# Sixteen short score matmuls of the sample rows, spread over the K tiles of projection block u6

## The chip, the cores and the metric

The kernel runs on one core of one Trainium2 chip. The time is that of one launch on the device, in microseconds (us). The engines named here are PE (the TensorE matmul; PEld is its weight load, which is recorded apart), DVE (VectorE), ACT (ScalarE), POOL (GpSimd) and SP (SyncE, which issues nearly all DMAs here, in order). Each engine works through its own list of instructions and waits on semaphores for the others.

## What is computed

One step of a decoder layer for a prompt group (16 meta tokens and 512 prompt positions) and for a sample group (8 rows, one new position each, with a cache of 128 keys and values per row). Cut to what matters:

```python
def mixer_inputs(h, pos, w_in, b_in):            # h: 2048 wide
    z = jnp.einsum('btd,de->bte', h, w_in) + b_in
    q, k, v, u = ...                             # 16 heads x 64, 4 x 64, 4 x 64, pool input 1024
    return partial_rope(q, pos), partial_rope(k, pos), v, u

def sink_attention(q, k, v, mask, sinks):
    s = jnp.einsum('...qhgd,...shd->...hgqs', q, k) * (1.0 / math.sqrt(HEAD_DIM))
    s = jnp.where(mask, s, NEG_INF)
    m = jnp.maximum(jnp.max(s, -1, keepdims=True), sink)
    p = jnp.exp(s - m)
    denom = jnp.sum(p, -1, keepdims=True) + jnp.exp(sink - m)
    return jnp.einsum('...hgqs,...shd->...qhgd', p / denom, v)

hs = layer_norm(x_sample, ...)
qs, ks_, vs, us = mixer_inputs(hs, pos_s, w_in[l], b_in[l])
k_all = jnp.concatenate([cache_k[l], ks_], 1)    # 128 cached keys and the new one
a_s = sample_window_attention(qs, k_all, v_all, pos_s, sinks)
```

After the mixer come the pooling branch, the output projection, a layer norm, a SwiGLU feed-forward block and a second layer norm, the same for both groups. The prompt rows and the sample rows share every large matmul: the 536 columns of a projection are 16 meta tokens, 8 sample rows and 512 prompt positions.

## The kernel before

All large products are computed in two float32r parts: a weight tile is split into `wh` (its rounded part, ACT, line 187) and `wl` (the rest, DVE, line 188), the activations likewise, and `products` issues wh·hi (L203), wh·lo (L204) and wl·hi (L206). Such a matmul is called wide below: a 128x128 weight against 276 or 260 columns. Small products, among them everything of attention, are plain float32 matmuls; the trace shows each of them as two passes.

The first stage (to about 350 us) makes the input projection. `in_block` computes 128 output features for all 536 columns: it takes two PSUM banks (276 and 260 columns) and calls `full_block`, which walks over the 2048 inputs in 16 K tiles; a K tile is six wide matmuls. Blocks q0 to q7 are query heads, u0 to u7 the pool input. Between the blocks stand the turns of attention. For turn t the program issues the values of turn t-1 (`att_values`, L609), the scores (`att_scores`, L547), one or two projection blocks, then the transposes of the softmax (`att_turn`, L591 to L598). The softmax runs on DVE and ACT meanwhile.

The sample rows' attention is a generator, `sample_attention`, cut into pieces by `yield`. Its first piece loads the cached keys (two tiles of 128x1024, `kct`) and makes the scores: for each of 8 rows and 2 halves of the heads, one matmul with a 128x128 tile of keys as weight and only 8 query columns (L697), 16 in all, into one PSUM bank `smT`. ACT copies the bank to SBUF (L699). Later pieces transpose it (L708), make the softmax, load the cached values (`vc`) and multiply by them with 32 short matmuls of 4 columns (L742).

`with step(pe)` fixes the order of groups on PE: what is issued in one step comes after what the step before issued. Within a step, and on the other engines, a scheduler orders the instructions. The loads of weights, of `kct` and of `vc` go through one ring of five raw tiles in the order in which the program asks for them; the two `vc` tiles come into the places of the two `kct` tiles. A place is free again when its last reader is done.

In turn 6 the first piece of `sample_attention` is asked for right behind the scores of the prompt; then block u6 follows:

```python
sc = att_scores(t, qs.pop(t))
if t >= 6:
    next(sample)
```

## Time and profile before

| | us |
|---|---|
| three timed runs | 1918.43, 1920.60, 1920.91 (median 1920.6) |
| the profiled execution, its own time | 1923.03 |
| span of its trace, first to last instruction | 1921.2 |
| PE busy in the span | 1890.5 (98%) |
| DVE busy | 1537.7 (80%) |
| ACT busy | 957.6 (50%) |
| mean granted clock of PE | 0.993 |

The trace belongs to the profiled execution alone, which took 2.43 us more than the median of the timed runs. Its times start at the first instruction. PE's busy time is modelled: a matmul is shown from its start to the end of its pipeline, so back-to-back matmuls overlap in the record, and what one costs is read from the distance of two starts. The granted clock (PEclk) is the share of full speed that TensorE was allowed in a stretch.

### The profile page before, as it was taken

What the parts mean: (1) busy time and instruction counts of PE and PEld (TensorE: products, weight loads), DVE (VectorE), ACT (ScalarE), POOL (GpSimd) and SP (SyncE); (2) the same over time, 40 slices, a digit from 0 to 9 for tenths busy, and PEclk for the clock granted to TensorE, in tenths of its full rate; (3) what the DMA queues carried; (4) which work ended last, traced back from release to release, by engine and by line L of the source; (5) the groups of instructions that cost most, each with busy time, mean ns of one, the idle gap of its engine ahead of it and who ended that gap; (6) DMA issues with size and microseconds to landing.
All of it is one profiled execution on the core that took longest, in us unless ns stands there. A gap on an engine that the chain in (4) does not pass through costs nothing.

```text
span 1921.2 us, 39215 instructions
## 1 busy us (share of the span) xinstructions
PE 1890.5 (98%) x15533; PEld 1862.9 (97%) x15533; DVE 1537.7 (80%) x2734; ACT 957.6 (50%) x1808; POOL 2.7 (0%) x9
## 2 busy tenths in 40 slices
PE   8999999999999999999999999999999999999996
PEld 8999999999989999999999999999999999999996
DVE  6666667768777988988898888888877888888878
ACT  6644445545654555555555555555555433434341
POOL 0000000000000000000000000000000000000000
PEclk9999999999999999999999999999999999999998
DMA  8722222665745455454545344453568655645332
GB/s 281 233 99 68 70 75 71 206 207 193 251 153 176 150 171 172 148 183 145 176 149 172 128 164 151 153 169 127 178 243 322 233 197 178 219 166 191 94 100 90
DMA packets 145240, 319.27 MB, mean 166 GB/s; under 512 B 14288, under 2 KB 66232, under 8 KB 144952
## 3 DMA queue, kind: packets, MB, share of 16 engines
q1 hardware_dynamic: 144480, 315.71, 49.6%
q8 instruction: 122, 2.00, 0.4%
q10 hardware_dynamic: 576, 1.05, 0.2%
q14 instruction: 62, 0.51, 0.1%
HBM read 265.22 MB, written 54.03 MB: 166 GB/s over the span
## 4 chain that ended last, share of the span: by engine, by line
PE 92%; DVE 3%; DMA 2%; ACT 2%; issue 1%; SPq 0%; DVEq 0%; ACTq 0%
PE p_g L203 8%; PE p_g L204 8%; PE p_g L206 8%; PE p_u L203 7%; PE p_u L206 7%; PE p_u L204 7%; PE tri L203 6%; PE tri L206 6%; PE tri L204 6%; PE o L203 3%; PE o L206 3%; PE o L204 3%; PE p_u L1003 2%; PE mm_u L203 2%; PE mm_u L206 2%; PE mm_u L204 2%
## 5 line engine op out<-in xcount | busy, mean ns | idle before, releaser
L187 ACT CAST rr<-fr 128x512 fp32r<-128x512 f32 (+1 forms) x1056 | 669.9, 644 | 738.3 <-DVE fr L196 151.5
L188 DVE TENSOR_TENSOR rr<-fr,rr 128x512 fp32r<-128x512 f32 (+1 forms) x1056 | 743.7, 715 | 244.2 <-ACT rr L187 233.8
L196 DVE TENSOR_TENSOR fr<-fr 128x1024 f32<-128x1024 f32 (+1 forms) x304 | 319.2, 1050 | 4.9 <-DMA fr<-in_w_g_dram 4.3
L203 PE MATMUL p_g<-rr 128*128 128x260 f32 x830 | 234.1, 283 | 0.0
L206 PE MATMUL p_g<-rr 128*128 128x260 f32 x830 | 230.2, 282 | 0.0
L204 PE MATMUL p_g<-rr 128*128 128x260 f32 x788 | 221.4, 282 | 0.0
L203 PE MATMUL p_u<-rr 128*128 128x260 f32 x770 | 217.8, 283 | 0.6 <-ACT fr L1044 0.6
L206 PE MATMUL p_u<-rr 128*128 128x260 f32 x770 | 214.7, 281 | 0.0
L204 PE MATMUL p_u<-rr 128*128 128x260 f32 x748 | 210.5, 282 | 0.0
L206 PE MATMUL tri<-rr 128*128 128x260 f32 x696 | 196.7, 283 | 1.8 <-DVE rr L188 1.8
L203 PE MATMUL tri<-rr 128*128 128x260 f32 x696 | 197.1, 283 | 0.8 <-ACT rr L187 0.8
L204 PE MATMUL tri<-rr 128*128 128x260 f32 x696 | 196.7, 283 | 0.0
L203 PEld LDWEIGHTS p_g<-rr 128*128 128x128 f32 x830 | 156.1, 188 | 0.0
L206 PEld LDWEIGHTS p_g<-rr 128*128 128x128 f32 x830 | 155.1, 189 | 0.0
L204 PEld LDWEIGHTS p_g<-rr 128*128 128x128 f32 x788 | 148.1, 188 | 0.0
L203 PEld LDWEIGHTS p_u<-rr 128*128 128x128 f32 x770 | 144.8, 188 | 0.8 <-ACT fr L1044 0.8
L203 PE MATMUL o<-rr 128*128 128x260 f32 x512 | 145.0, 284 | 0.3 <-ACT rr L187 0.3
L206 PEld LDWEIGHTS p_u<-rr 128*128 128x128 f32 x770 | 144.4, 189 | 0.0
L204 PE MATMUL o<-rr 128*128 128x260 f32 x512 | 144.0, 282 | 0.0
L206 PE MATMUL o<-rr 128*128 128x260 f32 x512 | 143.6, 282 | 0.2 <-DVE rr L188 0.2
L204 PEld LDWEIGHTS p_u<-rr 128*128 128x128 f32 x748 | 140.6, 188 | 0.0
L206 PEld LDWEIGHTS tri<-rr 128*128 128x128 f32 x696 | 131.3, 189 | 2.6 <-DVE rr L188 2.6
(320 smaller groups left out, 4563.2 us busy)
## 6 DMA issues: line engine op xcount, KB each, us to landing
fr<-in_w_u_dram SPq DMA_DIRECT2D x100, 512.0 KB
fr<-in_w_g_dram SPq DMA_DIRECT2D x90, 512.0 KB
fr<-in_w_d_dram SPq DMA_DIRECT2D x64, 640.0 KB
t_d<-fr SPq DMA_DIRECT2D x140, 260.0 KB
fr<-in_w_o_dram SPq DMA_DIRECT2D x64, 512.0 KB
fr<-in_w_in_dram SPq DMA_DIRECT2D x48, 512.0 KB
rr<-t_d SPq DMA_DIRECT2D x87, 260.0 KB
mid_b<-t_d SPq DMA_DIRECT2D x53, 260.0 KB
```

Source lines behind the costliest of these rows:

```text
L187: nc.scalar.copy(wh, s)
L188: last_lo[0] = (lo or nc.vector).tensor_sub(wl, s, wh.bitcast(F32)).ins
L196: i = op(*args).ins
L203: nc.tensor.matmul(o, wh, hi[j], start=first, stop=False, skip_group_check=onto)
L204: nc.tensor.matmul(o, wh, lo[j], start=False, stop=False, skip_group_check=onto)
L206: nc.tensor.matmul(o, wl, hi[j], start=False, stop=last, skip_group_check=onto)
L1003: nc.tensor.matmul(bk, self.q(0, n - 1)[:, k * P:(k + 1) * P], z1[0][4 * (n - 1) + k // 2][:, k % 2, :], start=(k == 0), stop=(k == 7))
```

## The change

`full_block` takes an optional generator `side` and advances it once behind each K tile. `u_block` and `in_block` pass it on, and only block u6 is given one: `sample`. The first piece of `sample_attention` is cut up: one `yield` stands behind the loads of the keys, and one behind each of the 16 score matmuls. So the call in turn 6 that made all scores now only asks for the keys, the 16 K tiles of u6 then each issue one score matmul, and a new call behind block u6 issues the copy of `smT` and the short products on DVE. The value products (L742) stay one run.

```diff
-    def full_block(src, name, out, hi, lo, low=None, apart=False):
+    def full_block(src, name, out, hi, lo, low=None, apart=False, side=None):
...
                          k == 0, k == KT - 1)
+                if side is not None:
+                    next(side)
...
                    for i in range(2)]
+            yield
             st_ = aux_tile([P, 2, 8, NS], "pt", "smT", 1)
             for b in range(NS):
                 kc = kcs[b // 4][:, b % 4]
                 for t4 in range(2):
                     ts = slice(4 * t4, 4 * t4 + 4)
                     nc.tensor.matmul(st_[:, :, ts, b], kc[:, t4, :], qd[:, :, ts, b], start=True, stop=True)
+                    yield
...
-                    us.append(u_block(int(n[1]), n == "u7"))
+                    us.append(u_block(int(n[1]), n == "u7", sample if n == "u6" else None))
...
             block(names[0])
+            if t == 6:
+                next(sample)
             with step(pe):
                 if t < 7:
                     att_turn(t)
```

In the changed file, line numbers are larger by 2 to 6 (L697 becomes L700, L699 becomes L703).

The order of PE before, from the last prompt scores of turn 6 (`sc`) over the short scores (`smT`) into block u6 (`mm_u`):

```order
L547 MATMUL sc_1_0_3256<-mid_a 128x256
L547 MATMUL sc_1_1_3257<-mid_a 128x256
L697 MATMUL smT<-fr 128x2x4 x16
L203 MATMUL mm_u_0_3326<-rr 128x276
L204 MATMUL mm_u_0_3326<-rr 128x276
L203 MATMUL mm_u_1_3327<-rr 128x260
L204 MATMUL mm_u_1_3327<-rr 128x260
L206 MATMUL mm_u_0_3326<-rr 128x276
L206 MATMUL mm_u_1_3327<-rr 128x260
L203 MATMUL mm_u_0_3326<-rr 128x276
```

The same place of PE after the change:

```order
L549 MATMUL sc_1_0_3256<-mid_a 128x256
L549 MATMUL sc_1_1_3257<-mid_a 128x256
L203 MATMUL mm_u_0_3305<-rr 128x276
L204 MATMUL mm_u_0_3305<-rr 128x276
L203 MATMUL mm_u_1_3306<-rr 128x260
L204 MATMUL mm_u_1_3306<-rr 128x260
L206 MATMUL mm_u_0_3305<-rr 128x276
L206 MATMUL mm_u_1_3306<-rr 128x260
L700 MATMUL smT<-fr 128x2x4
L203 MATMUL mm_u_0_3305<-rr 128x276
```

The run of 16 ahead of the block is gone; one short matmul stands behind every six wide ones, the last of them behind the last K tile and ahead of the transposes. Nothing else on PE moves.

The order of SP's DMAs before, at the loads of the cached values (`vc`), with what each waits for:

```order
L180 DMA fr<-in_vc_dram 128x1024 [waits DMAHW3_49,PE_49]
L180 DMA fr<-in_vc_dram 128x1024 [waits PE_49]
L180 DMA fr<-in_w_pool_dram 128x512 [waits DMAHW6_49,DVE_49]
L180 DMA fr<-in_w_o_dram 128x1024 [waits DMAHW1_49,DVE_49]
L663 DMA out_dram<-fr 15x128 [waits DMAHW7_49,Activation_49]
```

And after the change:

```order
L180 DMA fr<-in_vc_dram 128x1024 [waits DMAHW3_49,PE_49]
L180 DMA fr<-in_w_pool_dram 128x512 [waits DMAHW6_49,DVE_49]
L180 DMA fr<-in_w_o_dram 128x1024 [waits DMAHW1_49,DVE_49]
L180 DMA fr<-in_vc_dram 128x1024 [waits PE_49]
L665 DMA out_dram<-fr 15x128 [waits DMAHW7_49,Activation_49]
```

Each `vc` load waits for PE, which must have read the `kct` tile whose place it takes. The second one now stands behind a pool weight and the first output-projection weight.

On ACT the copy of `smT` stood ahead of four weight casts (L187):

```order
L573 ACTIVATE fr<-fr 128x2 x2
L699 COPY fr<-smT 128x128
L187 CAST rr<-fr 128x512 x4
L593 COPY mid_a<-tp_0_3448 16x256
L594 COPY mid_a<-tp_0_3448 128x256
```

After the change it stands behind them and ahead of the copies of the transposes:

```order
L575 ACTIVATE fr<-fr 128x2 x2
L187 CAST rr<-fr 128x512 x4
L703 COPY fr<-smT 128x128
L595 COPY mid_a<-tp_0_3448 16x256
L596 COPY mid_a<-tp_0_3448 128x256
```

So the copy, which needs all 16 score matmuls, no longer stands in front of the casts. On DVE a weight split moves past three short scalings of the softmax; POOL is unchanged.

## The prediction

> **What bounds the kernel now.** I read the page first, then the chain, then the stretch that the change touches.

> ```profile
> span 1921.2 us, 39215 instructions
> ...
> PE 1890.5 (98%) x15533; PEld 1862.9 (97%) x15533; DVE 1537.7 (80%) x2734; ACT 957.6 (50%) x1808; POOL 2.7 (0%) x9
> ...
> PE 92%; DVE 3%; DMA 2%; ACT 2%; issue 1%; SPq 0%; DVEq 0%; ACTq 0%
> ```

> PE is busy for 98% of the span and is 92% of the chain that ended last. Little stands between PE and the end, so a microsecond that PE loses or gains at 300 us should reach the end nearly whole. The waits of PE over the whole span say the same; its two longest groups are these:

> ```profile
> PE to L1406 <- DVE fr L236: 3.2, 1, 3.2
> PE tri L206 <- DVE rr L188: 2.4, 5, 0.7
> ```

> The first is at the very end, the second five waits in the down projection. Both are waits for engines that run behind PE's own progress, not for a clock of their own, so they move along when PE is early.

> The question is then what the run of short matmuls costs PE. The run itself, by the tile that it writes:

> ```profile
> L697 PEld LDWEIGHTS smT<-fr x32: 187/192/337, 295.3 to 299.5; 128*128 128x128 f32 x32
> L697 PE MATMUL smT<-fr x32: 256/256/362, 295.3 to 299.6; 128*128 128x8 f32 x32
> ```

> 16 matmuls are 32 passes (float32 takes two), each with its own weight load of 128x128 for 8 columns. The durations spread: 192 ns is the median weight load, 337 ns the longest. That is a change of clock, which the windows of that stretch show (columns: stretch, length, busy time and count of PE, PEld, DVE, ACT, POOL, then the granted clock, DMA share and GB/s):

> ```profile
> 294.53:297.94 3.41, 3.41 (x32) 3.03 (x30) 3.41 (x18) 0.85 (x4) 0.00 (x0) 1.00 0.28 101
> 297.94:301.35 3.41, 3.41 (x17) 3.41 (x18) 3.34 (x14) 3.41 (x16) 0.00 (x0) 0.50 0.63 167
> 301.35:304.77 3.42, 3.42 (x17) 3.42 (x17) 1.59 (x7) 1.03 (x6) 0.00 (x0) 0.50 0.38 140
> 304.77:308.18 3.41, 3.41 (x30) 3.41 (x29) 0.69 (x1) 0.79 (x2) 0.00 (x0) 1.00 0.17 41
> 338.90:342.31 3.41, 3.41 (x62) 2.74 (x60) 3.41 (x14) 0.54 (x2) 0.00 (x0) 1.00 0.53 155
> 342.31:345.73 3.42, 3.42 (x27) 2.86 (x26) 3.42 (x15) 2.75 (x8) 0.00 (x0) 0.50 0.88 268
> 345.73:349.14 3.41, 3.41 (x29) 3.21 (x29) 3.41 (x9) 3.41 (x12) 0.00 (x0) 1.00 0.83 277
> ```

> In the first window three quarters of the time are short passes. The granted clock falls to half at 297.94 and stays there for 6.83 us, two such windows, although the second is full of wide matmuls of u6. A second dip of one window, 342.31 to 345.73, follows the run of short value products, which the change leaves alone. [...]

> [...]

> **The change, part by part.** First the run, in its two clocks:

> ```profile
> 295.30:297.87 2.57, 2.57 (x23) 2.57 (x24) 0.00 (x0) 1.00 0.10 40
> 297.87:299.78 1.91, 1.91 (x11) 1.91 (x10) 0.00 (x0) 0.52 0.71 204
> ```

> 23 passes start in 2.57 us: 0.112 us each. The other 9 of the 32 take 1.91 us: 0.212 us each (the count of 11 takes in two that were still running). At full clock the run would take 32 x 0.1115 = 3.57 us; it takes 4.48. **The dip costs 0.91 us there.**

> Then u6 itself, by the starts of its K tiles:

> ```profile
> 299.78 0.58 PE L203 MATMUL mm_u<-rr 128*128 128x276 f32 x1
> ...
> 305.06 0.29 PE L203 MATMUL mm_u<-rr 128*128 128x276 f32 x1
> ...
> 313.96 0.27 PE L591 MATMUL tp<-fr,mid_a 128*16 128x128 f32 x1
> ```

> Four K tiles start between 299.78 and 305.06 (5.28 us), twelve between 305.06 and 313.96 (8.90 us, 0.742 each). At full clock four take 2.97 us. **The dip costs 2.31 us there**, 3.22 us in all.

> What the 32 short passes cost in their new places isn't shown, since no short float32 pass stands between wide ones. The nearest rows are one float32 matmul of full width between wide ones, in the output projection:

> ```profile
> 445.62 0.28 PE L206 MATMUL o<-rr 128*128 128x260 f32 x1
> 445.74 0.60 PE L872 MATMUL mean<-fr 128*128 128x260 f32 x2
> 445.99 0.48 PE L203 MATMUL o<-rr 128*128 128x260 f32 x1
> 446.30 0.29 PE L204 MATMUL o<-rr 128*128 128x260 f32 x1
> ```

> L206 to L872 is 0.12 us, the distance of any two wide ones: the weight load of a float32 pass hides behind a wide matmul. From L872 to L204 is 0.56 us: two passes and L203, which takes 0.12, so 0.22 a pass, and nothing for changing from float32 to float32r and back. In u6, then, the first pass of a pair finds its weights loaded, and two loads stay open: that of the second pass, behind 8 columns, and that of the next wide matmul, behind 8 columns. At the 0.112 us of the run a pair costs 0.223 us, 16 pairs 3.57 us, just what the run costs at full clock. Bounds: with one load of the two hidden too, 1.79 us less; with all three open, 1.79 us more. I take 3.57, the run's own pace.

> [...]

> Sum for PE from 295.30 to the transposes: before 18.66 us; after 16 x 0.742 + 3.57 = 15.44. **Gain 3.22 us**, if the clock stays full.

> Does it? A K tile with its pair takes 0.965 us, so a window of 3.41 us holds 21 wide matmuls. A window with as few exists in the down projection, where PE waited 0.79 us:

> ```profile
> 1468.71:1472.12 3.41, 2.62 (x22) 2.53 (x22) 2.17 (x3) 1.56 (x3) 0.00 (x0) 1.00 1.02 394
> ```

> 22 records (one of them from before the window) and the clock neither fell in it nor behind it. I count the dip as gone.

> The moved waits. The keys first:

> ```profile
> L180 SPq DMA_DIRECT2D fr<-in_kct_dram x2: 362/362/363, 253.2 to 259.7; - x2
> ```

> Their loads go out 35 us before the first score, so the waits of the score matmuls on them are met. For the rest:

> ```profile
> 302.14 0.24 ACT L699 COPY fr<-smT 128x128 f32<-128x128 f32 x1
> ...
> 315.93 0.38 PE L708 MATMUL smp<-fr 128*64 128x128 f32 x2
> ```

> ```profile
> 297.29 3.00 SPq L180 DMA_DIRECT2D fr<-in_vc_dram  x2
> 306.43 0.33 SPq L180 DMA_DIRECT2D fr<-in_w_pool_dram  x1
> 312.36 0.33 SPq L180 DMA_DIRECT2D fr<-in_w_o_dram  x1
> 316.84 0.36 SPq L663 DMA_DIRECT2D out_dram<-fr  x1
> ```

> ```profile
> 338.17 2.04 PE L742 MATMUL smo<-fr 128*64 128x4 f32 x64
> ```

> The copy of `smT` on ACT, 0.24 us, now follows the last score at about 310.7; its reader L708 stands 1.97 us of transposes behind u6 (313.96 to 315.93), which cover it. Without them the copy would cost PE some 0.5 us. Behind it in ACT's list stand copies of transposes that PE hasn't made by then. On SP the first `vc` load waits for half the pairs, until about 303, and holds up the pool weight, which went out at 306.43 and so isn't late. The second waits until 310.7, behind the output weight, and holds up only a store that waits for later work. The values are read at 338, some 24 us after. I take nothing for all of these; the work that hides them is u6 and block u7. DVE's one exchange lies in time that it idles.

> The sum against the profiled execution's own time: 1923.03 - 3.22 = 1919.8, with the second dip still in it. Against the median, which is 2.43 us lower, it depends on what the timed runs paid. If they paid the whole dip, 1920.6 - 3.22 = 1917.4. If the median run paid one window of half clock less (3.41 / 2 = 1.71), 1920.6 - 1.51 = 1919.1. Their own spread of 2.48 us fits dips that differ by a window or so. I take the middle, **1918.2 us**.

> **The rivals.**

> *The dip is a matter of where the windows fall.* The run is 3.57 us at full clock, a window 3.41. If a boundary cuts the run in two halves, neither window is three quarters short passes, and there may be no dip to remove. If most timed runs are so, the change gives nothing: **1920.6**. The spread of the three runs speaks for some such luck; against it stands that the median, not the lowest run, counts, and that two of three runs lie near the top. [...]

> *The clock falls for the whole block.* This one ends slower. If six wide matmuls and a pair are too little for the gate, it halves after the first window of u6 and the remaining 15.44 - 3.41 = 12.0 us take twice as long, and one more window passes before release (1.7): 1920.6 - 3.22 + 13.7 = **1931**. It decides at the array's share: 16 x 0.742 of 15.44, or 77%, must be too low. The row at 1468.71, with about as few wide matmuls, is against it.

> *A pair costs more between wide matmuls.* All three loads open: 1918.2 + 1.8 = **1920.0**. Against it the 0.12 us from L206 to L872.

> **How the numbers follow.** Dip gone and pairs at the run's pace: 0.74, 1916.4 to 1920.0 by the bounds. No dip to remove in the median run: 0.15. Pairs dearer: 0.07. Clock low for the block: 0.04. The range, 1916.2 to 1920.8, takes in the forecast with its bounds and the two rivals near it. 0.2% is 3.84 us, about what a measurement can tell from no change; the forecast gain of 2.4 is below it. Faster by more than that needs less than 1916.8, the low end of the forecast: 0.12. Slower by more needs the falling clock: 0.04. The rest, 0.84, is no difference.

> **What would show it.** Right: a granted clock of 1.00 from 295 to 311 us; pairs in u6 0.22 us apart from the wide ones, K tiles 0.965 us long; u6 done 15.4 us after the last prompt score; the copy of `smT` ahead of L708 without a wait of PE. The second dip may stay or go. Wrong: half clock inside u6, K tiles over 1.05 us (pairs dearer), or PE waiting for `smT`, `vc` or an output weight. If PE saves the 3.2 us and the time doesn't move, the timed runs before had no dip.

## The result, and the profile after

The changed kernel takes 1918.6 us (median of 20 runs, 1916.4 to 1920.9), the kernel before 1921.5 (20 runs, 1918.4 to 1922.8). The ratio is 0.9987 with an interval of 0.9981 to 0.9993: 2.5 us less, between 1.3 and 3.7 (the medians lie 2.9 us apart, the means 2.6). It is a real gain, and less than 0.2%.

The page of the changed kernel, its span, the busy times and the chain that ended last:

```profile
span 1919.0 us, 39213 instructions
...
PE 1887.9 (98%) x15533; PEld 1860.3 (97%) x15533; DVE 1537.8 (80%) x2734; ACT 957.2 (50%) x1808; POOL 2.7 (0%) x9
...
PE 93%; DVE 3%; ACT 2%; DMA 2%; issue 1%; SPq 0%; DVEq 0%; ACTq 0%
```

PE executes the same 15533 matmuls and is busy for 2.6 us less, and the span is 2.2 us shorter. The busy times of the other engines differ by 0.4 us at most. The windows over block u6 and over the second dip (columns as before: behind the busy times of the five engines stand the granted clock, the DMA share and GB/s):

```profile
295.92:299.33 3.41, 3.41 (x30) 3.08 (x27) 3.41 (x20) 1.11 (x6) 0.00 (x0) 1.00 0.18 70
299.33:302.74 3.41, 3.41 (x31) 3.41 (x30) 3.19 (x14) 3.41 (x14) 0.00 (x0) 1.00 0.00 0
302.74:306.16 3.42, 3.42 (x31) 3.42 (x30) 2.69 (x8) 1.76 (x6) 0.00 (x0) 1.00 0.23 49
306.16:309.57 3.41, 3.41 (x30) 3.41 (x30) 0.69 (x1) 0.62 (x1) 0.00 (x0) 1.00 0.56 186
...
336.88:340.29 3.41, 3.41 (x60) 2.74 (x58) 3.41 (x16) 0.65 (x3) 0.00 (x0) 1.00 0.50 154
340.29:343.70 3.41, 3.41 (x28) 2.80 (x24) 3.41 (x13) 3.19 (x9) 0.00 (x0) 0.50 0.87 265
```

Through u6 the clock stays at 1.00, with 30 or 31 records in each window; the second dip is still there in this execution. The timeline of PE in u6: its first wide matmul, two pairs and the K tile between them, and the first transpose behind the block:

```profile
296.43 0.39 PE L203 MATMUL mm_u<-rr 128*128 128x276 f32 x1
...
298.24 0.28 PE L700 MATMUL smT<-fr 128*128 128x8 f32 x2
298.37 0.37 PE L203 MATMUL mm_u<-rr 128*128 128x276 f32 x1
...
299.20 0.28 PE L700 MATMUL smT<-fr 128*128 128x8 f32 x2
...
311.88 0.27 PE L593 MATMUL tp<-fr,mid_a 128*16 128x128 f32 x1
```

From pair to pair it is 0.96 us, and the block takes 15.45. The last prompt score starts at 295.00 us before and at 296.13 after, from there to the transposes it takes 18.96 us before and 15.76 after: 3.20 less. The block began 1.13 us later in this execution: the clock was first released at 5.78 us (before at 4.39), after which PE was 0.66 us behind, and a wait of PE for ACT that ended at 17 us took 2.03 us instead of 1.56. So 2.1 us of the 3.2 show at the transposes and 2.2 in the span.

The moved waits, by the timelines of ACT, PE and SP:

```profile
312.26 0.26 ACT L703 COPY fr<-smT 128x128 f32<-128x128 f32 x1
...
313.85 0.38 PE L712 MATMUL smp<-fr 128*64 128x128 f32 x2
```

```profile
304.33 0.33 SPq L180 DMA_DIRECT2D fr<-in_vc_dram  x1
304.80 0.34 SPq L180 DMA_DIRECT2D fr<-in_w_pool_dram  x1
309.26 0.33 SPq L180 DMA_DIRECT2D fr<-in_w_o_dram  x1
312.06 0.33 SPq L180 DMA_DIRECT2D fr<-in_vc_dram  x1
```

The copy of the scores ends 1.3 us ahead of its reader, and each `vc` load goes out when the eight score matmuls that read its `kct` tile are done. The list of PE's waits is empty between 290 and 450 us.

### The profile page after: what moved, and what is told of

Read it like the earlier page. It is cut to its first block, busy times and chain, and to the rows that moved or that the text cites. A ratio compares the mean times of both kernels' runs of the same rounds, so it can differ in the third digit from the quotient of the medians.

```text
span 1919.0 us, 39213 instructions
## 1 busy us (share of the span) xinstructions
PE 1887.9 (98%) x15533; PEld 1860.3 (97%) x15533; DVE 1537.8 (80%) x2734; ACT 957.2 (50%) x1808; POOL 2.7 (0%) x9
## 3 DMA queue, kind: packets, MB, share of 16 engines
q10 hardware_dynamic: 576, 1.05, 0.2%
## 4 chain that ended last, share of the span: by engine, by line
PE 93%; DVE 3%; ACT 2%; DMA 2%; issue 1%; SPq 0%; DVEq 0%; ACTq 0%
PE p_g L203 8%; PE p_g L204 8%; PE p_g L206 8%; PE p_u L203 7%; PE p_u L206 7%; PE p_u L204 7%; PE tri L203 6%; PE tri L206 6%; PE tri L204 6%; PE o L203 3%; PE o L206 3%; PE o L204 3%; PE p_u L1009 2%; PE mm_u L203 2%; PE mm_q L203 2%; PE mm_u L206 2%
## 5 line engine op out<-in xcount | busy, mean ns | idle before, releaser
L187 ACT CAST rr<-fr 128x512 fp32r<-128x512 f32 (+1 forms) x1056 | 669.7, 644 | 734.7 <-DVE fr L196 152.5
L188 DVE TENSOR_TENSOR rr<-fr,rr 128x512 fp32r<-128x512 f32 (+1 forms) x1056 | 744.7, 716 | 239.1 <-ACT rr L187 228.6
L203 PE MATMUL p_g<-rr 128*128 128x260 f32 x830 | 234.1, 283 | 0.0
L206 PE MATMUL p_g<-rr 128*128 128x260 f32 x830 | 230.2, 282 | 0.0
L204 PE MATMUL p_g<-rr 128*128 128x260 f32 x788 | 221.4, 282 | 0.0
L203 PE MATMUL p_u<-rr 128*128 128x260 f32 x770 | 217.7, 283 | 0.2 <-ACT fr L1050 0.2
L206 PE MATMUL p_u<-rr 128*128 128x260 f32 x770 | 214.7, 281 | 0.0
L204 PE MATMUL p_u<-rr 128*128 128x260 f32 x748 | 210.5, 282 | 0.0
L206 PE MATMUL tri<-rr 128*128 128x260 f32 x696 | 196.8, 283 | 2.2 <-DVE rr L188 2.2
L203 PE MATMUL tri<-rr 128*128 128x260 f32 x696 | 197.1, 283 | 0.8 <-ACT rr L187 0.8
L204 PE MATMUL tri<-rr 128*128 128x260 f32 x696 | 196.7, 283 | 0.0
L203 PEld LDWEIGHTS p_g<-rr 128*128 128x128 f32 x830 | 156.1, 188 | 0.0
L206 PEld LDWEIGHTS p_g<-rr 128*128 128x128 f32 x830 | 155.1, 189 | 0.0
L204 PEld LDWEIGHTS p_g<-rr 128*128 128x128 f32 x788 | 148.1, 188 | 0.0
L203 PE MATMUL o<-rr 128*128 128x260 f32 x512 | 145.0, 284 | 0.3 <-ACT rr L187 0.3
L203 PEld LDWEIGHTS p_u<-rr 128*128 128x128 f32 x770 | 144.8, 188 | 0.4 <-ACT fr L1050 0.4
L206 PEld LDWEIGHTS p_u<-rr 128*128 128x128 f32 x770 | 144.5, 189 | 0.0
L204 PE MATMUL o<-rr 128*128 128x260 f32 x512 | 144.0, 282 | 0.0
L206 PE MATMUL o<-rr 128*128 128x260 f32 x512 | 143.6, 282 | 0.2 <-DVE rr L188 0.2
L204 PEld LDWEIGHTS p_u<-rr 128*128 128x128 f32 x748 | 140.6, 188 | 0.0
L206 PEld LDWEIGHTS tri<-rr 128*128 128x128 f32 x696 | 131.3, 189 | 3.0 <-DVE rr L188 3.0
```

The lines of the kernel that those rows point to most:

```text
L187: nc.scalar.copy(wh, s)
L188: last_lo[0] = (lo or nc.vector).tensor_sub(wl, s, wh.bitcast(F32)).ins
L203: nc.tensor.matmul(o, wh, hi[j], start=first, stop=False, skip_group_check=onto)
L204: nc.tensor.matmul(o, wh, lo[j], start=False, stop=False, skip_group_check=onto)
L206: nc.tensor.matmul(o, wl, hi[j], start=False, stop=last, skip_group_check=onto)
```

## The experiments

Three questions were open. Is it the clock, and what makes it fall? Does the dip lie the same in each execution? And would spreading the value products too bring the second dip down?

**Where the dip lies (e1, e4).** The kernel before, traced again without an edit.

> The kernel before, looked at once more, for where its half-clock windows fall. Theory (the clock is set window by window by how much of the window is short passes, and the grid of windows lies differently in each execution): the dip behind the run of short scores is there or not, and lasts 0, 1 or 2 windows of 3.41 us; from the first short score to the transposes behind u6 it takes 15.4, about 17.1 or about 18.7 us. Rival (the dip belongs to the kernel's order and not to the grid): 18.7 us again, two windows.

```profile
298.01:301.42 3.41, 3.41 (x31) 3.41 (x32) 3.41 (x17) 2.36 (x11) 0.00 (x0) 1.00 0.31 66
301.42:304.83 3.41, 3.41 (x18) 3.41 (x17) 2.46 (x10) 2.93 (x12) 0.00 (x0) 0.50 0.64 232
304.83:308.25 3.42, 3.42 (x29) 3.42 (x29) 1.65 (x5) 0.62 (x1) 0.00 (x0) 1.00 0.10 33
338.97:342.38 3.41, 3.41 (x68) 2.85 (x64) 3.41 (x12) 0.66 (x2) 0.00 (x0) 1.00 0.52 144
342.38:345.80 3.42, 3.42 (x28) 2.91 (x26) 3.42 (x17) 3.04 (x9) 0.00 (x0) 0.50 0.66 182
```

These windows show one window of half clock in u6 where the profiled execution had two. The run was over (its passes start from 297.27 to 300.75) when the clock fell at 301.42, so the next window was full of wide matmuls, and from 304.83 the clock is at 1.00 again. From the last prompt score to the transposes it takes 17.36 us: the dip costs 1.6, not 3.2. This is the middle case of the expectation. The second dip is there again.

> The kernel before, a third look. Theory (free-running grid): the dip begins at another place in the run of short scores than in the first and second look, and its cost (time from the first short score to the transposes, less 15.4 us) is 0 to 3.4 us. Rival (fixed by the order): the same place and 3.2 us again.

Half clock from 300.55 for one window, 17.36 us again, and a second dip at 341.51. The two windows and 3.2 us of the profiled execution are not fixed by the order of the program, so the rival is out. But the expectation of another place than in both traces ahead of it was only half met: the clock fell 2.64 us behind the first short pass in the profiled execution, 4.15 in e1 and 3.96 here, and the cost was 1.6 us in both of the latter.

**The run in the middle of u6 (e2).**

```diff
-                if side is not None:
-                    next(side)
+                if side is not None and k == 7:
+                    for _ in range(16):
+                        next(side)
```

> All 16 short scores in one run again, but in the middle of u6, behind its eighth K tile. Theory: the run is 3.57 us of short passes at full clock, so in most executions some window is mostly short passes and the clock halves inside u6 for 1 or 2 windows; from the start of u6 to the transposes 17 to 18.7 us instead of 15.45; the time 1.5 to 3 us above the changed kernel, near the kernel before. Rival (what matters is that the short passes no longer stand next to the prompt's scores and values, which use half of the array's rows or columns): no dip, 15.45 us, the time of the changed kernel.

```profile
300.31:303.73 3.42, 3.42 (x33) 3.42 (x31) 2.61 (x9) 3.42 (x13) 0.00 (x0) 1.00 0.03 8
303.73:307.14 3.41, 3.41 (x30) 3.41 (x31) 1.68 (x5) 0.27 (x1) 0.00 (x0) 1.00 0.80 235
307.14:310.55 3.41, 3.41 (x30) 3.41 (x29) 0.69 (x1) 0.62 (x1) 0.00 (x0) 1.00 0.44 145
```

The expectation of a dip missed in the traced execution: u6 takes 15.50 us at full clock. The windows show why it could: the run begins at 301.76 and the grid cuts it at 303.73, so that 1.97 us of one window (58%) and 1.5 us of the next (44%) are short passes. That left the rival standing. The median of ten runs is 1918.65, against 1921.12 of the kernel before on the same chip, but the ratio is 0.9993 (0.9983 to 1.0002), since the runs fall apart: six between 1917.4 and 1918.7, four between 1920.7 and 1922.8. Each run comes with its mean granted clock: 0.994 to 0.995 in the six, 0.992 to 0.994 in the four. By the means the four are 0.0019 lower, or 3.7 of 1920 us. That fits a dip in u6 in these four; where in the run their clock was low isn't recorded.

**Two runs of eight (e3).**

```diff
-                if side is not None:
-                    next(side)
+                if side is not None and k in (3, 11):
+                    for _ in range(8):
+                        next(side)
```

> The short scores in two runs of eight, behind K tiles 4 and 12 of u6: 1.79 us of short passes each. Theory (a window must be mostly short passes): at most 52% of a window is short passes, no dip, 15.45 us from the start of u6 to the transposes, the time of the changed kernel within 1 us. Rival (any run of over about a microsecond of short passes halves the clock): one or two dips, 17 to 19 us, the time of the kernel before.

```profile
299.40 1.85 PE L701 MATMUL smT<-fr 128*128 128x8 f32 x16
301.11 0.37 PE L203 MATMUL mm_u<-rr 128*128 128x276 f32 x1
```

The timeline of PE: half of the short passes in one run, 1.7 us to the next wide matmul, and no half clock in u6 nor behind it. From the last prompt score to the transposes 15.81 us; the median is 1918.3 (ratio 0.9986, 0.9976 to 0.9996), about that of the change, and all ten runs lie between 1916.7 and 1919.8. So a single short matmul behind each K tile isn't needed.

**Twice the short passes, spread (e5) and in one run (e6).** Both issue each score matmul twice; the second of the two also has the edit of the run in the middle. Each of e5, e6 and e7 ran once.

```diff
-                    nc.tensor.matmul(st_[:, :, ts, b], kc[:, t4, :], qd[:, :, ts, b], start=True, stop=True)
+                    for _ in range(2):
+                        nc.tensor.matmul(st_[:, :, ts, b], kc[:, t4, :], qd[:, :, ts, b], start=True, stop=True)
```

> Each short score is issued twice (the second writes the same numbers), still one pair of them behind each K tile of u6: 64 passes. Theory (a short pass costs 0.112 us wherever it stands, and the clock follows the share of short passes, here 38%): K tiles of 0.742 + 0.446 = 1.19 us, u6 takes 19.0 us from its first wide matmul to the transposes, the clock stays at 1.00. Rival (the weight loads of spread passes are partly hidden behind the wide ones): K tiles under 1.1 us, u6 under 17.5 us.

```profile
296.48 0.39 PE L203 MATMUL mm_u<-rr 128*128 128x276 f32 x1
...
298.50 0.51 PE L701 MATMUL smT<-fr 128*128 128x8 f32 x4
298.86 0.37 PE L203 MATMUL mm_u<-rr 128*128 128x276 f32 x1
...
299.69 0.28 PE L701 MATMUL smT<-fr 128*128 128x8 f32 x2
...
315.49 0.27 PE L593 MATMUL tp<-fr,mid_a 128*16 128x128 f32 x1
```

K tiles of 1.19 us, u6 19.01 us, full clock: 3.56 us for 32 more passes, 0.111 each, the pace of the run (0.112). So by the distances no load is hidden beyond the first of each group, which starts 0.12 us ahead of its pass (298.12 and 298.24 in the changed kernel).

> The same 64 passes, in one run behind K tile 8 of u6: 7.1 us at full clock, longer than two windows of 3.41 us. Theory: wherever the grid lies at least one window is short passes alone, so the clock halves within the run and u6 takes 1.7 to 5 us more than with the same passes spread: 20.7 to 24 us, half clock inside u6 for one to three windows. Rival (the place next to the prompt's scores made the dip, not the run): no half clock in u6, 19.0 us.

```profile
301.31:304.73 3.42, 3.42 (x32) 3.42 (x30) 2.61 (x9) 3.42 (x13) 0.00 (x0) 1.00 0.01 1
304.73:308.14 3.41, 3.41 (x33) 3.41 (x32) 1.85 (x6) 0.20 (x1) 0.00 (x0) 1.00 0.34 96
308.14:311.55 3.41, 3.41 (x19) 3.41 (x18) 0.00 (x0) 0.00 (x0) 0.00 (x0) 0.50 0.40 139
311.55:314.97 3.42, 3.42 (x16) 3.42 (x17) 0.00 (x0) 0.27 (x1) 0.00 (x0) 0.50 0.54 153
```

The same passes in one run: u6 takes 22.25 us, from 296.96 to 319.21, 3.24 more than spread, with two windows of half clock, and far from the prompt's scores. The two executions took 1922.71 us (e5) and 1926.30 (e6). This decides it against the rival that e2 had left standing: here a run made a dip without the prompt's scores beside it. The first window here, with 52% short passes (the run begins at 302.96), did not bring the clock down; the second, with nothing else, did.

**Eight times, spread (e7).** The same edit with `range(8)`.

> Each short score issued eight times behind its K tile, 256 passes: K tiles of 0.742 + 1.784 = 2.53 us, 71% of each window short passes, evenly. Looks for the share at which the clock falls. Theory: the trace of the run in the middle kept full clock with 58% short passes in a window, that of the kernel before lost it with 77%, so this share lies between: either full clock throughout (u6 takes 40.4 us) or half clock, in and out. Rival (only a window without wide matmuls, or nearly so, counts as idle): full clock, 40.4 us.

```profile
295.49:298.90 3.41, 3.41 (x31) 3.41 (x31) 3.41 (x18) 1.82 (x8) 0.00 (x0) 1.00 0.03 13
298.90:302.32 3.42, 3.42 (x32) 3.42 (x32) 2.54 (x11) 3.34 (x14) 0.00 (x0) 1.00 0.00 0
302.32:305.73 3.41, 3.41 (x18) 3.41 (x17) 1.79 (x7) 0.62 (x1) 0.00 (x0) 0.50 0.00 0
```

The first of these windows holds 1.95 us of short passes (57%, counted to the start of the next wide matmul) and the clock stays; the second 2.6 us (76%) and it falls. It then stays at half for 68.3 us, to the end of the block and 5 us past it, though every K tile brings its six wide matmuls: u6 takes 69.9 us instead of 40.4. The low clock stayed at a share that had not brought it down: the window from 302.32, at half clock, has 56% of short passes and isn't followed by a release. So spread passes kept full clock at 38% of the block (e5) and lost it at 71%, and the rival of the prediction, the clock falling for the whole block, exists at that share, against the change's 23%.

**The value products spread as well (e8)**: two behind each K tile of the second half of block u7; `mm` takes `side` as an argument, u7 passes it in its second half only, the bank comes from another ring, and the call behind `att_turn(7)` moves up:

```diff
-                    us.append(u_block(int(n[1]), n == "u7", sample if n == "u6" else None))
+                    us.append(u_block(int(n[1]), n == "u7", sample if n in ("u6", "u7") else None))
...
-            so = aux_tile([P, 8, NS], "pt", "smo", 1)
+            so = aux_tile([P, 8, NS], "o", "smo", 1)
...
                                          pT[:, j, 4 * t4:4 * t4 + 4, b], start=True, stop=True)
+                    yield
```

> The 32 short value products spread too: two behind each of the 16 K tiles of the second half of block u7, where only three wide matmuls make a K tile. Theory: the second dip (340 to 344 us in the changed kernel, up to 1.7 us) goes, but the 64 passes, which take 0.031 us each in their run since two of them load 64 columns each side by side, now leave the load of the next wide matmul open behind every K tile: about 0.19 us a K tile against 0.12, some 1 us more in all. The time within 1 us of the changed kernel, 2 to 3.5 us below the kernel before. Rival (the dip is all that counts): 1.7 us below the changed kernel in its median.

```profile
327.85 0.28 PE L206 MATMUL mm_u<-rr 128*128 128x260 f32 x1
328.06 0.28 PE L746 MATMUL smo<-fr 128*64 128x4 f32 x4
328.28 0.39 PE L203 MATMUL mm_u<-rr 128*128 128x260 f32 x1
328.51 0.28 PE L204 MATMUL mm_u<-rr 128*128 128x260 f32 x1
328.63 0.28 PE L206 MATMUL mm_u<-rr 128*128 128x260 f32 x1
328.84 0.28 PE L746 MATMUL smo<-fr 128*64 128x4 f32 x4
```

It takes 1921.8 us (ratio 1.0007, 0.9998 to 1.0016), 3 to 4 us more than the change (which was not run on this chip): both expectations missed. The trace has no second dip, but a K tile takes 0.77 us instead of 0.36 for its three wide matmuls: 0.41 us for four short passes, where about 0.19 was expected. From L206 to the first short pass it is 0.21 us, where a full-width pass follows after 0.12: the load of 64 columns starts only then, at 328.06, while the 128 columns of a short score are loaded from the start of the wide matmul ahead of it (298.12 in the changed kernel). On the way back L203 takes 0.23 us, and its load starts with it, at 328.28, so it isn't hidden either. Where all 64 stand in one run, in the kernel before, such loads start two by two, 6 to 7 ns apart, a pair every 58 ns. The 16 groups cost 16 x 0.41 = 6.6 us, against about 2.2 for the run.

**The run of value products kept whole, but among wide matmuls (e9)**, behind the eighth K tile of that half (the last edit, with the 16 calls made at once at `k == 7`), beside the changed kernel itself (e10).

> The changed kernel, with the run of short value products (64 passes, 1.97 us) kept in one but moved to behind the eighth K tile of the second half of block u7, about 3 us ahead of the transposes and values that it stood among. Theory (a window falls to half clock between 60% and 77% short passes; a run of 2 us with wide matmuls on both sides is at most 58% of a window; one run leaves only one change between half-array and full-array weights, unlike the run with both spread): no second dip, PE's work the same within 0.2 us, from the transposes of turn 6 to the mean of the layer norm 130.2 us instead of 131.8; the time 0 to 1.6 us below the changed kernel, about 1 in the median. Rival (moving the value products makes PE wait, or each change of weights costs more): above the changed kernel.

> The changed kernel once more, on the chip of the run before this one and with its runs of the kernel before, to compare the two. Theory: 2 to 3.5 us below the kernel before; K tiles of u6 0.965 us and full clock through u6; a second dip of one window between 335 and 345 us or none, by where the grid lies.

The moved run takes 1919.3 us (ratio 0.9992, 0.9984 to 1.0001), the change on the same chip 1918.5 (0.9989, 0.9980 to 0.9998). The change lies 2.4 us below the kernel before by the medians, as expected. No second dip in either trace, and the moved run is no faster. The list of PE's waits shows new ones:

```profile
PE pm L203 <- DVE mid_a L644: 0.4, 1, 0.4
PE pm L203 <- ACT rr L657: 0.3, 1, 0.3
```

From the transposes of turn 6 to the layer norm's mean it takes 131.5 us (130.2 was expected), 0.9 more than in the trace of the change beside it (130.6). The pool products wait for the split that DVE and ACT make of u7's result; in its old place the run stood ahead of these products, and there was no such wait. The waits account for 0.6 of the 0.9 us (0.35 and 0.29 in the timeline).

**The second dip (e11, e12).** Both kernels once more.

> The kernel before, a fourth look, for the second dip. In nine traces so far the window behind it fell to half clock whenever the run of value products began at 0.77 to 0.93 of a window of the grid (4 of 4) and not when it began at 0.30 to 0.54 (0 of 5). Theory (the first dip ends on the grid, and from its end to the value products the program takes 33.4 to 33.9 us, or 9.8 to 9.9 windows, so the first dip brings the second with it): if there is a first dip, the value products begin 33.3 to 34.0 us behind its end and a second dip follows. Rival (the two dips are independent): another phase, or no second dip after a first one.

First dip from 299.82 for one window, the value products 33.78 us behind its end, a second dip: as expected.

> The changed kernel, a third look. Theory: no half clock in u6, so nothing ties the value products to the grid; a second dip if they begin at over about 0.6 of a window, none if they begin below, and over the looks at kernels without a first dip fewer than half have one. Rival (independent dips, as frequent as before): a second dip again at any phase.

```profile
334.37:337.78 3.41, 3.41 (x78) 3.22 (x77) 3.41 (x11) 2.15 (x6) 0.00 (x0) 1.00 0.46 154
337.78:341.20 3.42, 3.42 (x37) 2.59 (x37) 3.42 (x18) 1.44 (x4) 0.00 (x0) 1.00 0.79 248
```

Here the run of value products begins at 335.69, at 0.39 of a window of the grid, and its last pass starts at 337.53, so it lies whole in the first of these windows (58%). Neither window brings the clock down, as expected. The execution took 1917.96 us.

## Why the prediction was right

**The dip and its removal**: right. The clock stays at 1.00 from 296 to 311 us, and the same 64 passes halved the clock for two windows in one run (e6, u6 22.25 us) and not spread (e5, 19.01 us).

**The price of a pair between wide matmuls**: taken as 0.223 us from the run's own pace, bounded by 1.79 us on either side for all 16. K tiles were to be 0.965 us and u6 15.44; they are 0.96 and 15.45, and doubling the pairs adds 0.111 us a pass. The bounds were far wider than needed; the row of L872 and the pace of the run had the answer.

**The moved waits, taken at nothing**: right, by the rows of ACT and SP above and by PE's list of waits, which is empty there.

**Carried to the end**: right. From the transposes of turn 6 to the layer norm's mean both profiled executions take 131.78 us, and from there to the end of the span 1475.4 (before) and 1475.3.

**The size against the median**: forecast 2.4 us, measured 2.5 by the ratio. That it came out so near is in part luck: the forecast was the middle of two cases, and neither is what the runs show. The profiled execution had two windows of half clock in u6; the three further traces of the kernel before had one, 1.6 us. So the second case fits better, that the median run paid one window less, and 1920.6 - 1.5 = 1919.1 would have been the sum by it. The second dip, which the sum left as it was, can give the rest: all four traces of the kernel before have it, of the three of the changed kernel one has. It costs 1.2 to 1.6 us (131.78 against 130.2 to 130.6 from the transposes to the mean). The prediction had allowed for that ("may stay or go") without a price. The timed runs have no trace, but each has a mean granted clock: on the chip of e9 and e10 the mean is 0.9934 over 21 runs of the kernel before and 0.9946 over 11 of the changed one. 0.0013 of 1920 us is 2.4 us, and the means of these times differ by 2.3. So over these executions the gain has the size of what the clock gave; how it divides between the two dips isn't shown.

**The rival that there is no dip to remove in most runs**: it had 0.15, and 0 of 4 traces show it. These four are not independent, though. Nine of the 14 traces, three of the kernel before and two of the changed one among them, also have one to three windows of half clock between 18 and 56 us, behind windows in which PE waited (26 to 59% busy). In e1, e4 and e11 the last of these dips ends 241.6 to 241.8 us, or 70.8 windows, ahead of the first short score, so the run met the grid at nearly the same place in all three. How many executions without these early dips would have none in u6 stays open. **The clock falling for the whole block** (the gate of this rival is whatever sets the granted clock): shown at 71% short passes (e7), not at the change's 23%.

## What to carry to other kernels

Look for dips of the granted clock as well as for waits: PE showed as busy throughout, and the profiled execution lost 3.2 us there without a wait of PE. The short matmuls that load 128x128 weights for 8 columns did better among wide ones (2.5 us less); the clock held where they filled up to 58% of a window of 3.41 us, and groups of 1.7 us did as well as single ones. Those that load 64 columns did not: a group of four passes among wide ones cost 0.41 us, against 0.14 for four in one run, so the run was better. Look at the neighbours of a run, too: the second dip came with 34 to 51% short passes.

## What the runs showed of the hardware

The share of short passes doesn't explain the second dip. The windows that brought it hold only 34 to 51% short value passes (34% in the changed kernel: 1.2 us of the window from 336.88); the rest of that window is 0.9 us of wide pool products and 1.3 us of the prompt's values, which also use weights of 64 columns (L611). Windows that held the whole run of value products (58%) between transposes and pool products kept the clock (e2, e6, e7, e10, e12). Which part of the mixture counts wasn't tested.

In the four traces of the kernel before a second dip came with the first. The changes of the clock lie on a grid of windows: in the profiled execution it is 37.54 us from the end of the first dip (304.77) to the start of the second (342.31), eleven windows of 3.41 us. From the end of the first dip to the value products the kernel before took 33.40, 33.70, 33.90 and 33.78 us, which puts their start at 0.79 to 0.93 of a window, so that the thin stretch behind it falls into one window. In the eight traces of kernels that left this stretch alone and had no dip in u6, or one that ended elsewhere (e6, e7), it began at 0.77 of a window once, with a dip, and at 0.24 to 0.54 seven times, without. That the first dip ties the second to the grid fits all twelve; the start of the program relative to the grid wasn't controlled, so the share of executions of the changed kernel that keep a second dip stays open.
